# Five gate groups as Strassen-type block products, forgetting softmax divided later, attention's halves added in DRAM: a hybrid decoder block on one core

## The chip, the core and the metric

The kernel runs on one core of a Trainium2 chip. The metric is the time of one execution on the device in microseconds; here it is the median of three runs. The engines work side by side and are named as in the profile: PE (matrix products), PEld (its loads of the stationary operand), DVE and ACT (vector and scalar engines), POOL and SP (which in this kernel mostly issue transfers; POOL also does a few elementwise operations). PSUM holds eight banks of 128 x 512 float32, into which PE writes.

## The reference

One decoder block over 1024 tokens of width 1024. Three attention branches are computed from one normalised input, each is multiplied by a sigmoid gate, and the sum goes through an output projection and a squared-ReLU MLP.

```python
proj = jnp.einsum('bsd,de->bse', h, w_in[l])
sb_q, sb_k, sb_v, fx_q, fx_k, fx_v, f_logit, m_q, gate_logit = split_columns(proj, SPLITS)
o_sb = stick_breaking_attention(...)      # 8 heads of 64
o_fox = forgetting_attention(...)         # 8 heads of 64, causal softmax with a decay
o_mem = memory_attention(mq, mk, ...)     # 4 heads of 128 over 256 memory tokens
gates = jax.nn.sigmoid(gate_logit.reshape(b, s, N_BRANCH, D_MODEL))
merged = gates[:, :, 0] * br_sb + gates[:, :, 1] * br_fox + gates[:, :, 2] * br_mem
x = x + jnp.einsum('bsd,de->bse', merged, w_out[l])
h2 = rmsnorm(x, g_mlp_norm[l])
u = jax.nn.relu(jnp.einsum('bsd,df->bsf', h2, w_ff_up[l]))
x = x + jnp.einsum('bsf,fd->bsd', u * u, w_ff_down[l])
```

`gate_logit` is a product of 1024 tokens x 1024 inputs x 3072 columns. The kernel writes its transpose to DRAM: 24 gates of 128 columns each.

## The kernel before

**Precision.** Every float32 operand is split into a high and a low part (`split`: ACT copies the high part, DVE subtracts), and every product is three matmuls (`passes`, high x high, high x low, low x high).

**Planner.** Up to the last branch, and again in a later part, the program is written as processes (`Op`, `Get`, `Sleep`, events) that a small simulated machine runs while the kernel is built. Each `Op` names an engine and a cost in microseconds; the order in which the machine starts them becomes the order of instructions on that engine. On the chip each engine runs its instructions in that order, each waiting for what it needs. An `Op` marked `side` on PE goes behind all others that are ready: the dense products are filler between attention's. `late` shifts a process's place among those that are ready. `Get` takes a buffer from a list (`Places`) and waits until one is free.

**Stages.** The prologue normalises and transposes the tokens (`hTh`, `hTl`: the transposed input, high and low, as 8 chunks of 128 inputs x 1024 tokens). Then come the values of the forgetting heads, two gates and the memory keys and values. Then six projections (`unit_products`, `PROJ`), each 512 columns, already done in seven block products: the 1024 inputs and 512 columns of the weights and the 1024 inputs and 1024 tokens are cut in halves, sums of the weight blocks (`unit_prep`) and sums of the token blocks (`sums_T`, kept in `T_of` as `P5`, `P6`, `P7`, `P4`) are multiplied in kinds `P1` to `P7`, and the results are added on DVE and ACT. Their weight blocks are loaded on POOL's queue (`unit_loads`, L1322). Then attention: `sb_tile` and `fox_tile` make the weights of one 128-token tile of one head, `unit` turns them on PE, splits them and multiplies them by the values. `load_pairs` loads keys and queries on POOL's queue (L979). Beside attention, on PE, run 22 gates (`dense_gate`, `dense_T`): 2 halves of the tokens x 8 chunks x 3 passes each, their weights loaded (L1037) and split (L1029, L1030) one gate at a time into one of three weight pairs (`WP`); at the opening of pool `A2` one pair is turned into four tiles for attention, and two are left. A gate half is evicted by ACT into an `o` tile (L1530) and stored by SP (L1534). Then the three branches (`dense_branch`, `bring`): memory, stick-breaking, forgetting, each multiplied by its gate, read back from DRAM. Then the output projection and the MLP, which the change does not touch.

**Softmax of the forgetting heads** (`fox_tile`, `fox` in the names): for each chunk of up to 512 keys DVE adds the causal mask to the last 128 columns (L843), takes the maximum (L844) and its negative (L845), and ACT takes the exponential with the sum (L848). With two chunks, small DVE operations (L856 to L867) make a factor for each, and ACT multiplies the whole row by it (L871).

**Attention's output.** The values are a high and a low part beside each other, so the product has 128 rows: 64 of each. ACT copies the low rows (L939), DVE adds the high ones (L940), SP stores the sum (L942).

## Time and profile before

| what | us |
|---|---|
| three runs | 1706.46, 1706.36, 1706.93 |
| the profiled execution | 1706.93 |
| its span, first to last instruction | 1705.1 |
| last store of attention's output, start | 845.4 |
| last store of a gate, start | 851.8 |

The page gives busy time by engine, the span in slices, the chain of work that ended last, and groups of instructions by line, engine and tile, with the mean duration of one and the idle time of the engine in front of them. In a row such as `pp<-hi,whi` the first name is what is written and the others what is read. Matmuls overlap, so the mean duration of one is longer than the distance to the next.

### The profile page before, as it was taken

To read this page: it belongs to the slowest core of one execution; us is meant where nothing else is said; L and a number is where in the kernel's file an instruction comes from. 1 tells how busy PE (TensorE), PEld (TensorE's weight loads), DVE (VectorE), ACT (ScalarE), POOL (GpSimd) and SP (SyncE) were. 2 spreads that over 40 slices of the span, in tenths; PEclk is the share of its full clock that TensorE was granted. 3 is DMA by queue.
4 is the path that set the end of the run, shared out by engine and by line. 5 is a ranking of instruction groups with operands and counts; after the bars stand their busy time and mean duration, and the time that the engine had idled before them with its cause. 6 is when DMAs were issued, how large, how long until landed. Compare 5 with 4: busy or idle time off the path is not lost.

```text
span 1705.1 us, 25350 instructions
## 1 busy us (share of the span) xinstructions
PE 1691.7 (99%) x9186; PEld 1442.8 (85%) x9186; DVE 1346.3 (79%) x2321; ACT 886.8 (52%) x1635; POOL 256.0 (15%) x441
## 2 busy tenths in 40 slices
PE   9999999999999999999999999999999999999998
PEld 9998899998888888888888887878888887888887
DVE  7977678868999888888656898987777776788775
ACT  6445555556676798889733446533233344332331
POOL 0000000043322233241000011021211120000000
PEclk9999999999999999999999999999999999999999
DMA  7545444576544453553375642144444484554532
GB/s 242 162 144 191 135 124 149 157 245 187 160 128 123 113 176 112 183 164 110 100 238 168 217 179 94 56 162 141 156 153 149 142 289 180 195 206 148 198 123 74
DMA packets 131406, 271.72 MB, mean 159 GB/s; under 512 B 15761, under 2 KB 43409, under 8 KB 131281
## 3 DMA queue, kind: packets, MB, share of 16 engines
q1 hardware_dynamic: 99600, 169.94, 29.2%
q0 software_dynamic: 31680, 100.17, 19.5%
q8 instruction: 72, 1.18, 0.3%
q14 instruction: 54, 0.43, 0.1%
HBM read 181.44 MB, written 88.60 MB: 158 GB/s over the span
## 4 chain that ended last, share of the span: by engine, by line
PE 83%; issue 7%; DVE 5%; DMA 2%; POOL 2%; ACT 1%; SPq 0%; POOLq 0%; DVEq 0%; ACTq 0%
PE pp L1119 21%; PE pp L2518 7%; PE pp L1405 7%; PE pp L1848 6%; PE sc L1405 5%; PE tr L904 4%; PE tr L2518 4%; PE sc L2518 4%; PE sc L1119 3%; PE sc L1848 3%; PE pv L2518 2%; PE pv L921 2%; PE pp L921 2%; PE pv L1405 2%; POOL s_scr L1865 2%
## 5 line engine op out<-in xcount | busy, mean ns | idle before, releaser
L1119 PE MATMUL pp<-hi,whi 128*128 128x512 f32 x368 | 147.6, 401 | 0.0
L1119 PE MATMUL pp<-hi,wlo 128*128 128x512 f32 x368 | 145.0, 394 | 0.0
L1119 PE MATMUL pp<-lo,whi 128*128 128x512 f32 x368 | 144.8, 393 | 0.0
L1030 DVE TENSOR_TENSOR wlo<-raw,whi 128x1024 fp32r<-128x1024 f32 (+1 forms) x82 | 100.0, 1221 | 38.9 <-ACT whi L1029 38.6
L2518 PE MATMUL pp<-h,sop 128*128 128x512 f32 x540 | 128.7, 395 | 1.4 <-DVE sop L1784 1.4
L2518 PEld LDWEIGHTS pp<-h,sop 128*128 128x128 f32 x540 | 101.1, 187 | 26.5 <-DVE sop L1784 1.8
L1848 PE MATMUL pp<-h,oh 128*128 128x512 f32 x384 | 120.9, 396 | 0.7 <-ACT cu L1934 0.6
L1029 ACT ACTIVATE whi<-raw 128x1024 fp32r<-128x1024 f32 (+1 forms) x82 | 86.8, 1059 | 52.4 <-PE pp L1405 18.7
L911 DVE TENSOR_TENSOR ptl<-tr,pth 128x512 fp32r<-128x512 f32 (+1 forms) x160 | 98.8, 627 | 11.0 <-ACT pth L909 10.6
L909 ACT ACTIVATE pth<-tr 128x512 fp32r<-128x512 f32 (+1 forms) x160 | 86.7, 558 | 28.5 <-PE tr L904 15.5
L814 DVE TENSOR_TENSOR_SCAN r<-r,sm 128x896 f32<-128x896 f32 (+4 forms) x64 | 85.5, 1345 | 3.5 <-ACT r L799 3.4
L2436 ACT ACTIVATE h<-t 128x2048 fp32r<-128x2048 f32 x16 | 30.7, 1919 | 110.4 <-DVE t L1784 97.9
L1848 PEld LDWEIGHTS pp<-h,oh 128*128 128x128 f32 x384 | 71.7, 187 | 19.2 <-ACT cu L1934 1.5
L1119 PEld LDWEIGHTS pp<-hi,wlo 128*128 128x128 f32 x368 | 69.1, 188 | 16.4
L1119 PEld LDWEIGHTS pp<-lo,whi 128*128 128x128 f32 x368 | 69.5, 189 | 10.3
L1119 PEld LDWEIGHTS pp<-hi,whi 128*128 128x128 f32 x368 | 69.4, 189 | 10.1
L1848 PE MATMUL pp<-h,ol 128*128 128x512 f32 x192 | 75.9, 396 | 0.0
L1841 ACT ACTIVATE oh<-raw 128x512 fp32r<-128x512 f32 x64 | 39.4, 625 | 61.7 <-DVE raw L1784 61.7
L2518 PE MATMUL sc<-h,sop 128*128 128x512 f32 x264 | 63.4, 395 | 0.0
L2518 PE MATMUL tr<-h,sop 128*128 128x512 f32 x264 | 63.4, 395 | 0.0
L1784 DVE TENSOR_TENSOR sop<-ur,sop 128x2048 fp32r<-128x2048 f32 x27 | 61.7, 2286 | 1.7 <-ACT sop L2447 1.7
L844 DVE TENSOR_REDUCE st<-sc 128x1 f32<-128x512 f32 (+2 forms) x96 | 53.3, 555 | 9.3 <-PE sc L838 7.1
(586 smaller groups left out, 5102.9 us busy)
## 6 DMA issues: line engine op xcount, KB each, us to landing
ur<-s_scr SPq DMA_DIRECT2D x26, 1024.0 KB
raw<-w_in POOLq DMA_DIRECT2D x42, 512.0 KB, 5.2
raw<-w_up SPq DMA_DIRECT2D x60, 256.0 KB
s_scr<-s POOLq DMA_DIRECT2D x60, 256.0 KB, 2.5
g<-w_down SPq DMA_DIRECT2D x14, 1024.0 KB
s_scr<-cu POOLq DMA_DIRECT2D x48, 256.0 KB, 2.9
gate_scr<-o SPq DMA_DIRECT2D x44, 256.0 KB
o<-gate_scr SPq DMA_DIRECT2D x32, 256.0 KB
```

The source lines that it names most:

```text
L814: nc.vector.tensor_tensor_scan(out=rev, data0=rev, data1=zero.to_broadcast([P, n]), initial=1.0, op0=ALU.mult, op1=ALU.add)
L904: nc.tensor.transpose(tr[:, jj * 256 + a * P:jj * 256 + (a + 1) * P], es[a][:, j * P:(j + 1) * P], ident)
L909: yield Op("ACT", act_time(512 - lo_c), lambda: nc.scalar.activation(ph[:, lo_c:], tr[:, lo_c:], AF.Copy))
L911: yield Op("DVE", dve_time(512 - lo_c), lambda: nc.vector.tensor_tensor(pl[:, lo_c:], tr[:, lo_c:], f32(ph[:, lo_c:]), ALU.subtract))
L921: nc.tensor.matmul(pv[0][:, c_:256], pair.v[:, j, b, :], p_[:, jj * 256 + c_:(jj + 1) * 256], start=(k == 0 and n_ == 0 and i == 0), stop= ...
L1029: yield Op("ACT", 0.03 + act_time(m), lambda: nc.scalar.activation(hi, raw, AF.Copy))
L1030: yield Op("DVE", dve_time(m), lambda: nc.vector.tensor_tensor(lo, raw, f32(hi), ALU.subtract))
L1119: nc.tensor.matmul(ps, a_, b_, start=(first and i == 0), stop=(last and i == n - 1))
L1405: nc.tensor.matmul(out_, a_, b_, start=(first and n == 0 and j == 0), stop=(last and n == 3 and j == len(todo) - 1), skip_group_check=True)
L1784: nc.vector.tensor_tensor(out_, a_, b_, op)
L1848: nc.tensor.matmul(ps, w[a_][:, k * P:(k + 1) * P], h[b_][k], start=(first and k == 0 and i == 0), stop=(last and k == 3 and i == 2), skip ...
L2518: nc.tensor.matmul(ps, a_[:, c, qs], b_[:, c, :], start=(kind in ("P1", "P2", "P7") and c == 0 and i == 0), stop=(kind in ("P2", "P4", "P3 ...
```

## The change

**Gates.** Of the 24 gates, 20 form five groups of 512 columns (`GATES`); two others (10 and 11) stay as they were, and gates 8 and 9 are done earlier as before. A group is done in seven block products of 2 x 4 x 3 = 24 matmuls (`gate_unit`), in three stages over all five groups: `P2` of all; then `P5` and `P3`; then `P1`, `P6`, `P7` and `P4`. Within a stage the kinds of one group accumulate in the same two banks, and after each kind ACT copies the running sum out (`evicted`), which is stored in the gate array by SP, or added to it by an accumulating transfer on POOL. The quarters of `hTh` and `hTl` that a stage has used up are overwritten with the token sums (`bring_T`), which were kept in DRAM (`keep_T`). The sums of weight blocks are made in DRAM beforehand (`gate_sums`): copies and accumulating transfers on POOL, with a load, a change of sign on ACT and a store where a block is subtracted.

**Gate sigmoids.** The gates of the memory branch were passed through the sigmoid at eviction; now they are stored without it, and it is applied when they are read back.

**Softmax.** Scores of the forgetting heads come negated (the sign moves into the query gain and the decay), so that a minimum gives the bias of the exponential directly; mask and minimum of the last chunk are one DVE instruction. The second chunk waits for the first one's minimum and uses the common one; the first is corrected by one DVE product over 512 columns. The rows are no longer divided by their sums: the reciprocals are stored (`sums_kept`), and `bring` of the forgetting branch loads them spread over 64 rows each and multiplies the attention output by them.

**Halves.** ACT copies all 128 rows of the output; SP stores the two halves to two arrays, and when a pair of heads is over, one accumulating transfer on POOL adds the low array to the other (`pair.added`).

**Buffers.** `bring` takes its raw tile from `RR` in place of `RAW`, and its first two tiles no longer wait for the branch to be chosen.

The core of the diff:

```diff
+    GATES, DIVIDED = (4, 5, 0, 1, 3), ()
...
+    def sums_kept(h0):
+        cols = fn[:, 8 * h0:8 * h0 + 16]
+        yield Op("DVE", SMALL, lambda: nc.vector.reciprocal(cols, cols))
+        yield Op("SP", 0.4, lambda: nc.sync.dma_start(
+            l_scr[h0:h0 + 2, :].rearrange("h (i p) -> p (h i)", p=P), cols, allow_slow_non_contiguous=True), 4.0)
...
             def maxima():
                 if c + u == n:
-                    dg = sc[:, u - P:u]
-                    nc.vector.tensor_tensor(dg, dg, tri, ALU.add)
-                nc.vector.tensor_reduce(mx[:, ci:ci + 1], sc[:, :u], AX.X, ALU.max)
-                nc.vector.tensor_scalar(nx[:, ci:ci + 1], mx[:, ci:ci + 1], -1.0, None, ALU.mult)
+                    nc.vector.tensor_tensor_reduce(sc[:, :u], sc[:, :u], holder["later"][:, 512 - u:512], 1.0, -NEG,
+                                                   ALU.add, ALU.min, nx[:, ci:ci + 1])
+                else:
+                    nc.vector.tensor_reduce(nx[:, ci:ci + 1], sc[:, :u], AX.X, ALU.min)
...
+            if ci == 0:
+                machine.fire(first_max)
+            else:
+                yield first_max
+                bias = m
+                yield Op("DVE", SMALL, lambda: nc.vector.tensor_tensor(m, nx[:, 0:1], nx[:, 1:2], ALU.min))
...
-        yield Op("DVE", SMALL * (4 if two else 1), scale)
-        yield Op("ACT", act_time(*[u for _, _, u in ch]) + 0.0002 * n, scaled)
+            def scaled():
+                nc.vector.tensor_scalar(e[:, :512], e[:, :512], f, None, ALU.mult)
+                nc.vector.scalar_tensor_tensor(total, l[:, 0:1], f, l[:, 1:2], ALU.mult, ALU.add)
+            yield Op("DVE", dve_time(512) + SMALL, scaled)
...
-        yield Op("ACT", act_time(256), lambda: nc.scalar.activation(o, pv[0][HD:P, :256], AF.Copy))
-        yield Op("DVE", dve_time(256), lambda: nc.vector.tensor_tensor(o, o, pv[0][0:HD, :256], ALU.add))
+        yield Op("ACT", act_time(256), lambda: nc.scalar.activation(ob, pv[0][:, :256], AF.Copy))
...
+            rows = slice(pair.p * P, pair.p * P + P)
+            yield Op("POOL", 0.8, lambda: nc.gpsimd.dma_start(
+                scr[rows, :], low_scr[pair.kind != "sb"][rows, :], max_dma_last_dim=2048, accum_op=ALU.add), 4.0)
+            machine.fire(pair.added)
...
+    def gate_sums():
+        yield kv_over
+        def moved(dst, src, **kw):
+            yield Op("POOL", 0.9, lambda: nc.gpsimd.dma_start(dst, src, max_dma_last_dim=2048, **kw), 0.0)
+            yield Sleep(7.5)
+        def turned(u, key, dst):
+            raw = yield Get(RAW)
+            view = raw[:, :1024].rearrange("p (k n) -> p k n", k=4)
+            yield from moved(view, gate_block(u, key).rearrange("(k p) n -> p k n", p=P))
+            yield Op("ACT", act_time(1024), lambda: nc.scalar.activation(raw[:, :1024], raw[:, :1024], AF.Copy, scale=-1.0))
+            yield Op("SP", 0.1, lambda: nc.sync.dma_start(dst.rearrange("(k p) n -> p k n", p=P), view), 6.0)
+            RAW.put(raw)
+        def first(u):
+            yield from moved(ws_scr[u, "P5"], gate_block(u, "21"))
+            yield from moved(ws_scr[u, "P5"], gate_block(u, "22"), accum_op=ALU.add)
+        def rest(u):
+            s3, s2, s4 = (ws_scr[u, k] for k in ("P7", "P6", "P3"))
+            two = [spawn(turned(u, "21", s3)), spawn(turned(u, "22", s2))]
+            yield two[0]
+            yield from moved(s3, gate_block(u, "11"), accum_op=ALU.add)
+            yield two[1]
+            yield from moved(s2, s3, accum_op=ALU.add)
+            yield from moved(s4, s2)
+            yield from moved(s4, gate_block(u, "12"), accum_op=ALU.add)
+        evs = []
+        for u in GATES:
+            evs += [spawn(first(u)), spawn(rest(u))]
+            yield Sleep(25.0)
...
+        def evicted(kind, q, ps, last, snapped):
+            yield last
+            gt = yield Get(OO)
+            yield Op("ACT", act_time(512), lambda: nc.scalar.activation(gt, ps, AF.Copy))
+            machine.fire(snapped)
+            if kind == kinds[-1]:
+                PP.put(ps)
+            (c, t), add = TO[kind]
+            r0 = u * 512 + c * 256 + q * P
+            dst = gate_scr[r0:r0 + P, t * 512:(t + 1) * 512]
+            if add:
+                yield Sleep(1.0)
+                yield Op("POOL", 0.9, lambda: nc.gpsimd.dma_start(dst, gt, accum_op=ALU.add), 4.0)
+            else:
+                yield Op("SP", 0.1, lambda: nc.sync.dma_start(dst, gt), 2.7)
+            OO.put(gt)
...
+                for q in range(2):
+                    if j == 0:
+                        banks_.append((yield Get(PP)))
+                    else:
+                        yield snapped[q]
...
-    gates = [dense_gate(n, may_gate) for n in (*range(16, 24), *range(0, 8), *range(10, 16))]
+    plain = [dense_gate(n, may_gate) for n in (*range(16, 24), *range(0, 8), *range(10, 16)) if n // 4 not in GATES]
+    stage = [[gate_unit(u, kinds, may_gate if i == 0 else (lambda: sums_in.fired)) for u in GATES]
+             for i, kinds in enumerate((("P2",), ("P5", "P3"), ("P1", "P6", "P7", "P4")))]
+    gates = plain + stage[0] + stage[1] + stage[2]
...
+        spawn(gate_sums(), -10.0)
+        spawn(keep_T(), 2.0)
+        spawn(bring_T("P5", plain))
+        spawn(bring_T("P6", stage[0]))
+        spawn(bring_T("P7", stage[1]))
+        spawn(bring_T("P4", stage[1]))
```

215 lines of the change are left out of this document (161 added, 54 removed).

## The prediction

> **What bounds the kernel now.** I read the page first, then the windows of busy time by stage, then the lines and waits of the one stage that the change touches.
>
> ```profile
> span 1705.1 us, 25350 instructions
> PE 1691.7 (99%) x9186; PEld 1442.8 (85%) x9186; DVE 1346.3 (79%) x2321; ACT 886.8 (52%) x1635; POOL 256.0 (15%) x441
> PE 83%; issue 7%; DVE 5%; DMA 2%; POOL 2%; ACT 1%; SPq 0%; POOLq 0%; DVEq 0%; ACTq 0%
> ...
> 115.00:365.00 250.00, 250.00 (x1800) 234.53 (x1799) 194.72 (x354) 129.39 (x205) 22.85 (x34) 1.00 0.49 155
> 365.00:600.00 235.00, 234.03 (x1355) 202.49 (x1354) 211.93 (x340) 164.96 (x357) 79.90 (x140) 1.00 0.54 155
> 600.00:851.00 251.00, 251.00 (x1514) 218.91 (x1513) 205.28 (x642) 212.21 (x546) 70.69 (x126) 1.00 0.46 140
> 851.00:1060.00 209.00, 207.29 (x908) 167.35 (x907) 162.99 (x241) 94.59 (x151) 16.81 (x17) 1.00 0.53 180
> ```
>
> The columns of a window row are its length, then PE, weight loads, DVE, ACT and POOL busy, the granted clock, the DMA share and GB/s. The first row is the projections, the next two are the attention stage (stick-breaking, then forgetting and memory attention), with the gates as filler on PE, and the last is the branches. PE is without a gap in all of them, at the full clock of 1.00. So one matmul less is worth its spacing, as long as nothing else opens a gap. The next engines are close: in the attention stage DVE is busy 417.2 of 486 us (86%, and 90% in its first half), ACT 377.2 us (78%).
>
> ```profile
> L942 SPq DMA_DIRECT2D o_scr<-ob x64: 445/446/559, 390.1 to 845.4; - x64
> ...
> L1534 SPq DMA_DIRECT2D gate_scr<-o x44: 319/326/328, 372.0 to 851.8; - x44
> ```
>
> These are the transfers that store the attention's outputs and the gates, with the start of the first and of the last. Attention ends at 845.4, the gates at 851.8: they end together. Attention's matmuls go first by the planner, so its pace is that of DVE and ACT, and the gates take what is left of PE. To end earlier, both must shrink.
>
> **The gates' products.** The gates' matmuls in this stage, and the spacing of twelve of them in the chain of waits:
>
> ```profile
> L1119 PE MATMUL pp<-hi,whi 128*128 128x512 f32 x352 | 141.3, 401 | 0.0
> L1119 PE MATMUL pp<-hi,wlo 128*128 128x512 f32 x352 | 138.7, 394 | 0.0
> L1119 PE MATMUL pp<-lo,whi 128*128 128x512 f32 x352 | 138.5, 393 | 0.0
> ...
> 366.20 2.78 PE pp L1119 x12
> ```
>
> 1056 matmuls are 22 gates of 48, at 2.78 / 12 = 0.232 us each (the mean of 0.39 to 0.40 us is a duration that overlaps its neighbours). A group of 512 columns costs 4 x 48 = 192 of them; by block products it costs 7 kinds x 2 halves x 12 = 168. Five groups save 5 x 24 = 120 matmuls, 120 x 0.232 = **27.8 us** of PE. No other stage loses or gains a matmul.
>
> **What the vector engines gain and lose in this stage.** The rows that go, and the two that price what comes:
>
> ```profile
> L844 DVE TENSOR_REDUCE st<-sc 128x1 f32<-128x512 f32 (+2 forms) x96 | 53.3, 555 | 9.3 <-PE sc L838 7.1
> L1030 DVE TENSOR_TENSOR wlo<-raw,whi 128x1024 fp32r<-128x1024 f32 x22 | 26.7, 1216 | 1.3 <-ACT whi L1029 1.2
> L843 DVE TENSOR_TENSOR sc<-sc,above 128x128 f32<-128x128 f32 x64 | 18.7, 292 | 6.8 <-PE sc L838 5.7 <-ACT pth L909 0.8
> ...
> L845 DVE TENSOR_SCALAR st<-st 128x1 f32<-128x1 f32 x96 | 14.7, 154 | 3.3
> L940 DVE TENSOR_TENSOR ob<-ob,pv 64x256 f32<-64x256 f32 x33 | 13.4, 405 | 7.6 <-ACT ob L939 7.5
> L940 DVE TENSOR_TENSOR ob<-ob,pp 64x256 f32<-64x256 f32 x31 | 12.4, 402 | 3.1 <-ACT ob L939 3.1
> ...
> L636 DVE TENSOR_SCALAR r<-r,st 128x256 f32<-128x256 f32 x32 | 9.5, 359 | 0.3
> L865 DVE TENSOR_SCALAR st<-st 128x2 f32<-128x2 f32 x32 | 7.3, 229 | 1.1
> L864 DVE RECIPROCAL st<-st 128x1 f32<-128x1 f32 x32 | 5.3, 164 | 1.1
> L863 DVE TENSOR_TENSOR st<-st 128x1 f32<-128x1 f32 x32 | 5.1, 160 | 1.1
> L867 DVE RECIPROCAL st<-st 128x1 f32<-128x1 f32 x32 | 4.9, 154 | 1.4 <-ACT es L848 1.4
> L862 DVE TENSOR_TENSOR st<-st 128x2 f32<-128x2 f32 x32 | 4.8, 151 | 2.5 <-ACT st L858 2.5
> ...
> L616 DVE TENSOR_SCALAR st<-st 128x2 f32<-128x2 f32 x16 | 2.8, 176 | 0.5
> ```
>
> DVE loses L843, L845, L940, L862 to L867 and L616: 18.7 + 14.7 + 25.8 + 27.4 + 2.8 = 89.4 us. It gains 15 more weight splits (35 blocks and 2 plain gates for 22 gates), 15 x 1.216 = 18.2; 32 products of 128x512 by a column, at 0.49 us by the slope between L865 (2 elements, 229 ns) and L636 (256, 359), or 0.68 if they run like a two-operand instruction of that size: 15.7 to 21.8; 32 small ones like L865, 7.3. The reduction that now adds the mask is not in the trace: between nothing (one instruction like L844) and 0.2 us (a separate read of the result, which ACT's row below has) on 64 tiles, 0 to 13; I take 6. Sum 41 to 60, so DVE goes down by 29 to 48 us, to 369 to 388. Over a stage of 486 - 28 = 458 us that is 81 to 85%: no worse than now.
>
> ```profile
> L871 ACT ACTIVATE e<-e,st 128x512 f32<-128x512 f32 x64 | 37.6, 639 | 2.7 <-DVE st L865 1.8 <-DVE st L856 0.6
> ...
> L1530 ACT ACTIVATE o<-pp 128x512 f32<-128x512 f32 x43 | 25.8, 601 | 13.3 <-PE pp L1119 13.2
> L1029 ACT ACTIVATE whi<-raw 128x1024 fp32r<-128x1024 f32 x22 | 23.4, 1063 | 3.8 <-DMA raw<-w_in 3.8
> L871 ACT ACTIVATE es<-es,st 128x128 f32<-128x128 f32 (+3 forms) x32 | 17.7, 561 | 0.6 <-DVE st L867 0.5
> ...
> L848 ACT ACTIVATION_READ_ACCUMULATOR e<-sc,st 128x1 f32 x64 | 12.8, 201 | 0.0
> ```
>
> ACT loses L871, 55.3 us, and gains 30 evictions (74 for 44), 18.0, and 15 splits, 15.9: 355.8 us, 78% of 458, as now. The relief lies in the forgetting half (DVE there loses some 76 us and gains 35); in the stick-breaking half L940's 12.9 us pays just for some ten more splits, so that half keeps its pace and the gates move 385 of their 936 matmuls into the second, which has 251 - 555 x 0.232 + 48 x 0.232 (memory attention's own 48 matmuls, by the code, are also on L1119) = 133 us of attention on PE and 89 us of gates, 222 for 251. Should attention lag behind the gates all the same, branch 0 (192 matmuls, 44.5 us, with operands from memory attention alone) fills PE. I cost the relief itself at nothing beyond the 27.8: PE sets the end. Without that relief DVE would be at 417 + 18 = 435 of 458 us, 95%, and attention would last as now.
>
> **The weights' cadence.** Three weight pairs exist, and one of them is given to attention's tiles, so two serve the gates. A pair in use for 48 matmuls now serves 24.
>
> ```profile
> 463.28 0.60 ACT L1530 ACTIVATE o<-pp 128x512 f32<-128x512 f32 x1 [0.32 <-PE pp L1119]
> ...
> 470.26 1.22 DVE L1030 TENSOR_TENSOR wlo<-raw,whi 128x1024 fp32r<-128x1024 f32 x1
> ...
> 365.00:600.00 235.00, 144.33 (x551) 1.00 0.54 155
> 600.00:851.00 251.00, 148.27 (x555) 1.00 0.46 140
> ```
>
> A gate's last matmul releases its pair at 463.3, and the pair is split again at 471.5: 8.2 us. L1119 takes 551 x 0.232 = 128 of 235 us in the first half, so a block of 24 (5.57 us alone) lasts 10.3 us there, and 13.9 in the second half (89 of 222). The refill fits with 2 us to spare. Bounds: nothing, and 1.2 us for each of 23 blocks (a refill of 11.5 us behind 30 more evictions), 28 us. I take **3 us**, near the measured refill.
>
> **The transfers in the projections.** The weight sums run on POOL from about 115 us on, the partial sums of the tokens on SP. Per group: 2 loads, 2 stores, 2 copies and 4 adding transfers of 512 KB; 26.2 MB for five groups, and 8.4 MB of token sums. ACT's ten sign changes (10 x 1.063) are hidden in its 121 us of idle time there.
>
> ```profile
> L1322 POOL DMA_DIRECT2D raw<-w_in x20 | 15.2, 760 | 282.5 <-DVE wlo L1030 282.5
> ...
> DMA to landing us min/median/max: 4.1/4.9/6.2
> ...
> 307.12 0.75 POOL L1322 DMA_DIRECT2D raw<-w_in  x1 [6.27 <-DVE wlo L1030]
> ...
> 319.09 1.21 DVE L1335 TENSOR_TENSOR s<-raw,raw 128x1024 f32<-128x1024 f32 x1
> ```
>
> What is queued behind them on POOL are the blocks of the projections' weights (L1322, the first two rows); the last two rows are the last block's issue and its first use, 12 us apart, so a landing of 4.9 us has 7 us to spare. The engines carry 155 GB/s at a share of 0.49, so 316 when full; 34.6 MB in 250 us are 138 GB/s, which makes a share of 0.93. No adding transfer is in the trace. Its cost is bounded by a plain one (4.9 us) from below, and from above by twice the bytes, a share of 1.06, with which the sums simply end later: their first use, after 2 plain gates and the five P2 blocks, is at about 365 + 41 + 51 = 457. The sums have time; what can be late are the blocks, by nothing or by 7 us a unit in 5 units (the slow rival). I take **3 us**.
>
> The Trainium skill, "Collectives: The Full Stack", section "The bandwidth ceiling: the fold count and why AG ≠ RS ≠ AR", says that an add in the transfer path needs two source reads and runs at half the rate of a copy. By it 4.9 us become an estimated 9.8; no run here shows it yet, and it is the side on which the slow rival lies.
>
> In the attention stage POOL gets 15 loads, 30 adding stores and 8 pair adds, 53 x 0.76 = 40 us on 151 busy, in 458: hidden in its waits. The last pair's add delays only branch 2's operand, with branches 0 and 1 in front of it. The 16 sigmoids of branch 0's gates (16 x 0.6) and its broadcast sums lie in the branch window, where ACT has 114 us idle.
>
> **Sum.** The profiled execution took 1706.93 us (span 1705.1, 1.8 around it; the median of the runs is 0.5 lower): 1706.9 - 27.8 + 3 + 3 = **1685 us**.
>
> **The rivals.** *Nothing lost*: 1679 us, the bare 27.8. For it: PE has no gap now. Against: twice the weight blocks and 53 more transfers in POOL's order.
>
> *The cadence decides*: each kind waits for its weights. If half of the 28 us bound comes true, 1706.9 - 27.8 + 14 + 3 = 1696; up to 1704 with more of it. For it: 2 us of room, DVE at 90% in the first half. Against: POOL issues loads well ahead, and the order of ACT and DVE is planned around them.
>
> *The blocks of the projections are late*, the case on the other side: adding transfers, each waiting on POOL for the landing of the one it depends on, hold back L1322, and a full set of DMA engines stretches its landing. It decides from a landing past 12 us; at 19 us each of the 5 later units waits 7, 35 us in all: 1706.9 - 27.8 + 35 = 1714. For it: the share of 0.93 to 1.06 if all runs in that stage. Against: POOL waits 282 us on this stage for releases, room for 40 issues, and the sums may run on until 457.
>
> *No effect*: the 27.8 come back as gaps at the end because attention paces the stage. Branch 0 as filler speaks against it; it would be 1706.
>
> **How the numbers follow.** Forecast, 1680 to 1692: 0.55. Nothing lost, below 1680: 0.08. Cadence, 1692 to 1705: 0.15. No effect: 0.02. Late blocks, above 1710: 0.20. A measurement of this kernel tells about 0.2% (3.4 us) from no change: faster 0.76 (all of the first three but 0.02), same 0.04, slower 0.20. The range 1677 to 1708 leaves out the slow rival.
>
> **What would show it.** Right: 936 matmuls in the gates' groups, PE without gaps until about 823 and the branches as before; DVE below 390 us in the attention stage; L1322 landing below 12 us. Wrong: PE idle in front of weight blocks with DVE's split as releaser (cadence); PE idle between 115 and 365 with L1335 behind a block's landing (late blocks); PE idle after the last gate while attention still stores (attention paces).

## The result, and the profile after

The changed kernel takes **1760.9 us** (median of four executions; 1752.5 to 1769.3), beside 1706.7 for the kernel before: 1.0314 times as long, with a 95% interval of 1.0294 to 1.0335. The forecast was 1685. The execution profiled here took 1764.6 us. From its page:

```profile
span 1762.9 us, 25226 instructions
...
PE 1686.6 (96%) x9066; PEld 1435.7 (81%) x9066; DVE 1311.5 (74%) x2072; ACT 877.8 (50%) x1610; POOL 336.7 (19%) x534
...
DMA packets 176894, 340.97 MB, mean 193 GB/s; under 512 B 27072, under 2 KB 71616, under 8 KB 175744
...
PE 72%; DMA 13%; DVE 6%; issue 4%; ACT 3%; POOL 2%; SPq 0%; ACTq 0%; POOLq 0%; DVEq 0%
```

The 120 matmuls are gone (9186 to 9066), but PE's busy time fell by 5.1 us and not by 27.8, and PE is idle 1762.9 - 1686.6 = 76.3 us where it was idle 13.4. In the chain of waits DMA has 13%, where it had 2%. So the span grew by 62.9 us of idle PE and fell by 5.1. The windows by stage, with the columns of the prediction's first fence, say where PE was idle and where its clock was lower:

```profile
115.00:365.00 250.00, 231.16 (x1594) 213.94 (x1593) 183.53 (x327) 130.21 (x198) 52.09 (x64) 0.97 0.89 250
365.00:600.00 235.00, 231.40 (x1427) 203.90 (x1427) 205.56 (x302) 165.09 (x360) 87.11 (x152) 1.00 0.77 233
600.00:851.00 251.00, 223.21 (x1320) 193.83 (x1320) 162.03 (x402) 167.62 (x447) 104.72 (x167) 0.94 0.82 190
851.00:920.00 69.00, 57.48 (x286) 46.83 (x285) 32.88 (x69) 36.29 (x79) 10.94 (x13) 0.93 0.85 164
```

PE lost 18.8 us in the projections and 39.3 us between 600 and 920 (27.8 and 11.5). No other engine is near its limit there: DVE is busy 65% between 600 and 851, ACT 67%. The granted clock is below 1.00 in the same stages: 1686.6 - (1691.7 - 27.8) = 22.7 us is what the same matmuls took more. The DMA share is 0.77 to 0.89, and between 600 and 920 at *fewer* GB/s than between 365 and 600. That is the first thing to look at.

**Four stores that fill the DMA engines.** The store of the reciprocals of the row sums, and the same execution in windows of 5 us around the first two of the four:

```profile
L603 SPq DMA_DIRECT2D l_scr<-fn x4: 376/378/387, 691.2 to 888.5; - x4
```

```profile
685.00:690.00 5.00, 5.00 (x32) 4.43 (x32) 4.96 (x13) 4.14 (x11) 5.00 (x11) 1.00 0.75 227
690.00:695.00 5.00, 5.00 (x30) 4.33 (x29) 3.36 (x12) 3.67 (x12) 3.11 (x5) 1.00 1.29 112
695.00:700.00 5.00, 5.00 (x33) 4.33 (x32) 3.67 (x9) 3.54 (x11) 3.59 (x6) 1.00 0.73 21
700.00:705.00 5.00, 3.47 (x23) 2.73 (x21) 0.75 (x2) 0.38 (x2) 0.52 (x1) 1.00 0.95 181
705.00:710.00 5.00, 0.99 (x5) 0.99 (x6) 1.49 (x2) 2.86 (x8) 1.57 (x3) 0.69 1.05 233
710.00:715.00 5.00, 5.00 (x18) 4.24 (x18) 4.02 (x12) 2.22 (x6) 2.30 (x5) 0.63 0.96 313
...
765.00:770.00 5.00, 2.88 (x17) 2.12 (x15) 1.31 (x5) 0.00 (x0) 0.94 (x2) 1.00 0.82 139
770.00:775.00 5.00, 0.00 (x0) 0.00 (x0) 0.00 (x0) 0.08 (x1) 2.44 (x4) 0.67 1.08 315
775.00:780.00 5.00, 2.43 (x6) 1.85 (x7) 2.89 (x5) 3.85 (x9) 0.00 (x0) 0.50 1.08 310
```

The store is issued at 691.2. For the next ten microseconds the DMA share (last column but one) stays at 1.29 and 0.73 while the engines move 112 and then 21 GB/s. Then the engines stop: from 700 on DVE and ACT do next to nothing, and soon PE too, idle for 1.5 and 4.0 us of two windows. It comes back at a clock of 0.63, so 18 matmuls fill a window that held 30 and more before. The second gap, at 770, is 9.7 us of three windows, with a clock of 0.50 in the last. Each gap is paid twice, as idle time and then as slow matmuls. The Trainium skill, "TensorE: Matmul & The Clock Gate", Part 1, says that an idle window of about 3.4 us takes the clock to half. These rows agree: the clock reads 0.50 behind the gap of 9.7 us.

How a late store stops engines that have nothing to do with it is in the chain of waits of that stretch (start, length, what):

```profile
693.31 13.75 DMA o_scr<-o
...
707.14 0.21 ACT o L685
...
707.64 0.60 ACT pth L918
...
708.26 0.70 DVE ptl L920
...
709.01 0.90 PE tr L913 x3
```

A store of 256 KB of the memory branch, next on SP's queue, lands after 13.75 us. ACT waits for its tile (L685) to copy the next bank; behind it in ACT's fixed order is attention's copy (L918), behind that DVE's split (L920), behind that PE's turn (L913), for which PE waits 5.5 us. The next matmuls of the gates stand behind that turn in PE's order, which is written down too. The second gap has the same form with another transfer: ACT waits 10.3 us to split a gate's weight block that has not landed, and PE waits 9.7 us for attention's exponential behind it.

**The projections.** The issue line of the weight blocks of the projections with their time to landing, the chain of waits in this stage, two instructions of ACT with the idle time in front of them (in brackets, with what ended it), the waits of PE between 115 and 365 (us in all, how often, the longest), and three windows of 10 us:

```profile
L1356 POOL DMA_DIRECT2D raw<-w_in x20: 748/780/1589, 131.2 to 336.1; - x20
...
DMA to landing us min/median/max: 4.5/8.1/13.9
```

```profile
176.09 0.75 POOL raw L1580
176.84 15.85 DMA raw<-w_in
...
192.71 0.03 ACT raw L1587
...
212.29 12.10 DMA raw<-w_in
...
243.53 11.09 DMA raw<-w_in
```

```profile
191.34 1.06 ACT L1587 ACTIVATE raw<-raw 128x1024 f32<-128x1024 f32 x1 [8.89 <-DMA raw<-w_in]
...
253.26 1.06 ACT L1587 ACTIVATE raw<-raw 128x1024 f32<-128x1024 f32 x1 [5.97 <-DMA raw<-w_in]
```

```profile
PE sc L1439 <- ACT sn L1478: 9.5, 1, 9.5
PE tr L716 <- DVE sn L708: 7.0, 3, 4.0
PE pp L1439 <- DVE wlo L1057: 0.9, 1, 0.9
PE pp L1153 <- DVE wlo L1057: 0.9, 1, 0.9
PE pp L1153 <- ACT whi L1056: 0.6, 1, 0.6
```

```profile
190.00:200.00 10.00, 0.78 (x2) 0.69 (x3) 2.51 (x4) 7.45 (x8) 3.22 (x4) 0.74 1.12 283
250.00:260.00 10.00, 5.98 (x38) 5.78 (x37) 4.55 (x14) 6.58 (x12) 3.13 (x4) 0.83 1.08 256
300.00:310.00 10.00, 10.00 (x88) 10.00 (x87) 9.73 (x23) 4.59 (x9) 0.00 (x0) 1.00 0.12 40
```

The blocks of the projections, which landed in 4.9 us, land in 8.1 (13.9 at most). But they are not what stops PE. The three transfers that hold the chain for 11 to 16 us are loads of the weight sums themselves (issued on L1580; the tile is named `raw` there too), and what waits for them is ACT's change of sign (L1587). In ACT's fixed order the projections' own work stands behind it. At 191 ACT has waited 8.9 us, then comes to the copy of a finished product out of PSUM (L1478), and PE, which needs that bank, has waited 9.5 us. At 253 ACT has waited 6.0 us, DVE's L708 needs a root that ACT takes behind it, and PE has waited 4.0. These two are 13.5 of the 18.8 us that PE lost in this stage; for split weight blocks it waited 2.4 us in all (the last three rows of its waits). The DMA share is 0.84 to 1.14 while the sums run and 0.12 at 300, when they are done: the stage's mean of 0.89 hides a full stretch with a much emptier one behind it.

### The profile page after: what moved, and what is told of

The parts are those of the page before. It is cut to its first block, busy times and chain, and to the rows that moved or that the text cites. A ratio compares the mean times of both kernels' runs of the same rounds, so it can differ in the third digit from the quotient of the medians.

```text
span 1762.9 us, 25226 instructions
## 1 busy us (share of the span) xinstructions
PE 1686.6 (96%) x9066; PEld 1435.7 (81%) x9066; DVE 1311.5 (74%) x2072; ACT 877.8 (50%) x1610; POOL 336.7 (19%) x534
## 2 busy tenths in 40 slices
DMA packets 176894, 340.97 MB, mean 193 GB/s; under 512 B 27072, under 2 KB 71616, under 8 KB 175744
## 4 chain that ended last, share of the span: by engine, by line
PE 72%; DMA 13%; DVE 6%; issue 4%; ACT 3%; POOL 2%; SPq 0%; ACTq 0%; POOLq 0%; DVEq 0%
PE pp L2056 9%; PE pp L1705 8%; PE pp L2726 7%; PE pp L1153 5%; PE sc L2056 4%; DMA raw<-w_in 4%; PE pp L1439 4%; PE tr L2726 3%; PE sc L2726 3%; PE sc L1153 3%; PE sc L1439 3%; DMA gate_scr<-o 3%; PE tr L913 3%; PE pv L2726 2%; PE tr L2056 2%
## 5 line engine op out<-in xcount | busy, mean ns | idle before, releaser
L1057 DVE TENSOR_TENSOR wlo<-raw,whi 128x1024 fp32r<-128x1024 f32 (+1 forms) x92 | 112.3, 1221 | 74.9 <-ACT whi L1056 74.8
L920 DVE TENSOR_TENSOR ptl<-tr,pth 128x512 fp32r<-128x512 f32 (+1 forms) x160 | 99.3, 630 | 37.2 <-ACT pth L918 35.2
L1056 ACT ACTIVATE whi<-raw 128x1024 fp32r<-128x1024 f32 (+1 forms) x92 | 97.4, 1060 | 57.3 <-DMA raw<-w_in 19.5
L1705 PE MATMUL pp<-hi,whi 128*128 128x512 f32 x280 | 114.6, 409 | 0.0
L1705 PE MATMUL pp<-hi,wlo 128*128 128x512 f32 x280 | 112.4, 401 | 0.7 <-DVE wlo L1057 0.7
L1705 PE MATMUL pp<-lo,whi 128*128 128x512 f32 x280 | 111.9, 400 | 0.0
L918 ACT ACTIVATE pth<-tr 128x512 fp32r<-128x512 f32 (+1 forms) x160 | 87.5, 566 | 31.5 <-PE tr L913 13.3
L825 DVE TENSOR_TENSOR_SCAN r<-r,sm 128x896 f32<-128x896 f32 (+5 forms) x64 | 85.5, 1348 | 3.2 <-ACT r L809 2.9
L913 PE MATMUL tr<-ident,e 128*128 128x128 f32 x416 | 62.6, 279 | 3.6 <-DVE ptl L920 3.0
L1673 ACT ACTIVATE o<-pp 128x512 f32<-128x512 f32 x70 | 42.2, 604 | 45.6 <-PE pp L1705 25.7
L1705 PEld LDWEIGHTS pp<-hi,wlo 128*128 128x128 f32 x280 | 53.6, 191 | 13.9 <-DVE wlo L1057 1.1
L2073 POOL DMA_DIRECT2D s_scr<-cu x48 | 26.0, 542 | 193.8 <-DVE cu L2063 190.0
## 6 DMA issues: line engine op xcount, KB each, us to landing
ws_P<-w_in POOLq DMA_DIRECT2D x20, 512.0 KB, 10.3
```

The source lines that it names most:

```text
L825: nc.vector.tensor_tensor_scan(out=rev, data0=rev, data1=zero.to_broadcast([P, n]), initial=1.0, op0=ALU.mult, op1=ALU.add)
L913: nc.tensor.transpose(tr[:, jj * 256 + a * P:jj * 256 + (a + 1) * P], es[a][:, j * P:(j + 1) * P], ident)
L918: yield Op("ACT", act_time(512 - lo_c), lambda: nc.scalar.activation(ph[:, lo_c:], tr[:, lo_c:], AF.Copy))
L920: yield Op("DVE", dve_time(512 - lo_c), lambda: nc.vector.tensor_tensor(pl[:, lo_c:], tr[:, lo_c:], f32(ph[:, lo_c:]), ALU.subtract))
L1056: yield Op("ACT", 0.03 + act_time(m), lambda: nc.scalar.activation(hi, raw, AF.Copy))
L1057: yield Op("DVE", dve_time(m), lambda: nc.vector.tensor_tensor(lo, raw, f32(hi), ALU.subtract))
```

## The experiments

Every ratio is to the kernel before, run beside it on the same chip. Steps between two runs are differences of ratios times 1706.7 us.

| run | median us | ratio, 95% interval |
|---|---|---|
| the changed kernel | 1760.9 | 1.0314 [1.0294, 1.0335] |
| e1 row sums turned on PE | 1723.5 | 1.0107 [1.0092, 1.0122] |
| e16 row sums in rows of 32 bytes | 1724.7 | 1.0101 [1.0084, 1.0118] |
| e2 no weight sums | 1739.4 | 1.0194 [1.0167, 1.0222] |
| e5 ordinary gate stores | 1746.3 | 1.0235 [1.0216, 1.0254] |
| e6 = e1 and no weight sums | 1708.2 | 1.0006 [0.9996, 1.0016] |
| e9 = e6 and ordinary gate stores | 1700.3 | 0.9963 [0.9949, 0.9977] |
| e13 = e6, token sums planned, not sent | 1698.1 | 0.9952 [0.9937, 0.9967] |
| e10 = e6 and no token sums | 1685.0 | 0.9869 [0.9849, 0.9889] |
| e11 = e10 and ordinary gate stores | 1683.1 | 0.9866 [0.9838, 0.9895] |
| e3 no block products | 1704.9 | 0.9992 [0.9982, 1.0001] |
| e7 = e3, row sums turned | 1705.7 | 0.9999 [0.9989, 1.0009] |
| e17 = e3, rows of 32 bytes | 1702.4 | 0.9982 [0.9973, 0.9992] |
| e4 = e1, weight sums at half pace | 1712.4 | 1.0036 [1.0019, 1.0053] |
| e8 = e4, token transfers spread | 1713.4 | 1.0038 [1.0023, 1.0053] |
| e14 = e4, token loads on ACT's queue | 1722.5 | 1.0095 [1.0080, 1.0110] |
| e15 = e4, planned for earlier landings | 1742.5 | 1.0218 [1.0200, 1.0235] |
| e12 = e4, planned for later landings | 1770.3 | 1.0365 [1.0338, 1.0392] |

### The row sums: e1 and e16

e1 turns the sixteen columns first, so that rows of 512 bytes are stored:

```diff
-            l_scr[h0:h0 + 2, :].rearrange("h (i p) -> p (h i)", p=P), cols, allow_slow_non_contiguous=True), 4.0)
...
+        yield Op("PE", 0.12, lambda: nc.tensor.transpose(tr[:16, :P], cols, ident))
...
+        yield Op("ACT", act_time(P), lambda: nc.scalar.activation(ob[:16, :P], tr[:16, :P], AF.Copy))
...
+            l_scr[h0:h0 + 2, :].rearrange("h (i p) -> (h i) p", p=P), ob[:16, :P]), 2.5)
```

> The changed kernel with one edit: the 16 columns of row sums are turned on PE, copied by ACT and stored as rows of 512 bytes, in place of the four stores of 4-byte elements. Theory A (each of the four stores holds the DMA engines for about 15 us, attention's own store behind it lands after 13.75 us, PE stands some 10 us and then runs at a granted clock of 0.5 to 0.7): the four gaps at 691, 755, 822 and 889 us go, about 12 us each with the clock, 48 in all: 1761 - 48 = 1713 us, clock back to 0.99 or more in the attention stage. Theory B (the weight sums fill the DMA engines in the projections, 16 us of PE idle there and as much again by the clock): this run changes nothing before 600 us, and the 16 us of idle between 140 and 300 stay. Rival (the gaps after 690 come from the gates' accumulating stores and the pair adds): they stay, 1755 to 1761 us.

e1 gained 2.07%, 35 us, where theory A had 48; the rival is out. Theory B held in so far as PE still loses 17 us in the projections. But the new steps made the planner write another order on every engine, so e16 was added later, with one line other and the order of all engines as it was:

```diff
-            l_scr[h0:h0 + 2, :].rearrange("h (i p) -> p (h i)", p=P), cols, allow_slow_non_contiguous=True), 4.0)
+            l_scr[h0:h0 + 2, :].rearrange("h (p i) -> p h i", p=P), cols.rearrange("p (h i) -> p h i", h=2)), 4.0)
```

> The changed kernel with one line other: the four row-sum stores write the same 8 KB each in rows of 8 elements (32 bytes), so 256 pieces for 2048, and the row sums lie in another order. Order and waits of all engines are those of the changed kernel. Theory A (the 2048 small pieces of each store): 1761 - 37 = 1724 us, DMA share behind the stores below 1.1, no gap at 705, 770, 825 and 905. Rival (the other order that the planner wrote for the turned row sums): 1752 us or more.

e16 gained 2.13%, **36 us**, from the same bytes in the same place. Its page, and the windows behind its first store (issued at 694.2):

```profile
DMA packets 169726, 340.97 MB, mean 198 GB/s; under 512 B 19904, under 2 KB 64448, under 8 KB 168576
```

```profile
695.00:700.00 5.00, 5.00 (x31) 4.33 (x30) 3.61 (x12) 4.41 (x14) 3.11 (x6) 1.00 0.93 189
700.00:705.00 5.00, 5.00 (x37) 4.52 (x35) 3.53 (x7) 3.80 (x10) 2.62 (x5) 1.00 1.02 240
705.00:710.00 5.00, 5.00 (x28) 4.26 (x27) 4.71 (x12) 3.44 (x10) 1.66 (x4) 1.00 1.05 299
```

There are 176894 - 169726 = 7168 packets less, which is 4 x (2048 - 256): each store was cut into one packet for each 4-byte element. With 256 pieces the engines carry 189 to 299 GB/s behind it and PE has no gap. The Trainium skill, "DMA: Bandwidth & Descriptors", "Rules for kernel authors", says that a last dimension that is not contiguous lowers to one descriptor per element; this run agrees and gives the price in this kernel.

### Without block products: e3, e7, e17

```diff
-    GATES, DIVIDED = (4, 5, 0, 1, 3), ()
+    GATES, DIVIDED = (), ()
...
-        spawn(gate_sums(), -10.0)
-        spawn(keep_T(), 2.0)
...
```

> The changed kernel with all gates computed plainly, so without block products, weight sums and token sums; the softmax relief, the pair adds in DRAM and the four row-sum stores stay. 120 matmuls of 0.232 us come back. Theory A: the projections are as in the kernel before and the four gaps are there: 1707 + 40 to 48 = 1747 to 1755 us. Rival (the gaps come from the gates' accumulating stores, which this run has not): no gaps, 1700 to 1708 us.

> The softmax relief and the pair adds alone, with turned row sums, all gates computed plainly. Theory (the four stores of 4-byte elements cost 3 us where the attention stage has room): 1704.9 - 3 = 1702 us, PE without the two gaps near 717 and 777. Rival (the relief is worth much and the stores hide it, as theory A had it): 1670 to 1680 us. Rival (PE sets the end, the stores cost nothing): 1705 us.

> The run with all gates computed plainly (1704.9 us, four stores of 4-byte elements in it), with the same one line other: rows of 32 bytes, the row sums in another order, all engines' orders as in that run. Theory (the same four stores cost next to nothing where PE has gates of 48 matmuls for each weight pair and little other traffic: two gaps of 1.5 us): 1702 to 1705 us. Rival (they cost here too, hidden by the relief): 1690 us or less.

e3 refuted theory A as it stood: with the same four stores the time is that of the kernel before. Rows of 32 bytes at an unchanged order on every engine gain 0.10%, under 2 us, where they gain 36 in the changed kernel. So the stores are not dear by themselves; they are dear in the kernel with the block products. Which part of those makes them so is not shown: the traffic, a weight pair that serves 24 matmuls in place of 48, or the order. (The adding stores are at most a small part of it: they cost 13 us beside the row-sum stores and 7 without those and the weight sums, as the next runs show.) In the windows of e3, behind its second store (issued at 700.6), the stall is there, and PE loses 1.5 us at a clock that stays at 1.00:

```profile
710.00:715.00 5.00, 5.00 (x33) 4.34 (x32) 3.46 (x10) 3.02 (x9) 1.99 (x3) 1.00 1.00 159
715.00:720.00 5.00, 3.53 (x23) 2.92 (x22) 2.07 (x4) 2.83 (x7) 1.07 (x2) 1.00 1.08 310
```

And the relief of DVE and ACT, with the pair adds in DRAM beside it, is worth nothing that can be told from no change (e7: 0.9999, as its last rival had it).

### The adding stores: e5 and e9

```diff
-                yield Op("POOL", 0.9, lambda: nc.gpsimd.dma_start(dst, gt, accum_op=ALU.add), 4.0)
+                yield Op("POOL", 0.9, lambda: nc.gpsimd.dma_start(dst, gt), 4.0)
```

> The changed kernel in which the gates' 30 adding stores are ordinary stores on the same queue, so the partial results of the gates are not added; the weight sums and the four row-sum stores of 4-byte elements stay. Without block products the same four stores cost 3 us of PE, with them 37. Theory D (the row-sum stores meet the adding stores, and it is the pair that fills the DMA engines: share 1.3 to 1.7 behind them): without adds the four gaps shrink to about 3 us and the time falls by some 30, to 1728 to 1735 us. Rival E (it is the rest: more traffic, and a weight pair that now serves 24 matmuls and not 48, so that the same stall of the DMA engines uncovers PE): the gaps stay, 1752 to 1761 us.

> Turned row sums, no weight sums, and the gates' 30 adding stores as ordinary stores, so the gates' partial results are not added. The run before it without the last edit took 1708 us, of which 16.7 us are PE idle more than in the kernel before and about 9 us matmuls at a lower clock. Theory F (an adding transfer loads the DMA engines more than a plain one of the same bytes, and that is what makes the other transfers late): 6 to 10 us less, 1698 to 1702 us, DMA share between 600 and 851 below 0.70. Rival G (it is POOL's order: the store waits there for its eviction, 92.7 us in all, and the weight blocks and attention's loads queue behind it, added or not): 1706 to 1709 us.

The order of all engines is unchanged in both. Beside the 4-byte stores the adds cost 0.79%, 13 us, less than the 30 expected of theory D, and not the nothing of rival E. Without those stores and the weight sums they cost 0.43%, 7 us, as theory F had it. The spans of e6 and e9, and the time that the packets of POOL's queue took:

```profile
span 1702.9 us, 25163 instructions
...
q0 software_dynamic: 40336, 120.09, 24.6%
```

```profile
span 1693.5 us, 25163 instructions
...
q0 software_dynamic: 38416, 120.09, 23.0%
```

The same 120.09 MB took 0.246 x 1702.9 - 0.230 x 1693.5 = 29.4 us of all 16 engines less: 0.98 us for each of 30 stores. By the prediction's 316 GB/s an ordinary store of 256 KB takes an estimated 0.83 us, so the add about doubles it. The rule that the prediction cited from the Trainium skill, "Collectives: The Full Stack", "The bandwidth ceiling: the fold count and why AG ≠ RS ≠ AR" (an add needs two source reads, which halves its rate beside a copy; stated there for the reducing step of a collective), agrees with it.

### The weight sums: e2, e6, e4

```diff
-                          [(0, gate_block(u, BLOCK[kind]) if kind in BLOCK else ws_scr[u, kind])], 4, 256))
+                          [(0, gate_block(u, BLOCK.get(kind, "21")))], 4, 256))
...
-    stage = [[gate_unit(u, kinds, may_gate if i == 0 else (lambda: sums_in.fired)) for u in GATES]
+    stage = [[gate_unit(u, kinds, may_gate) for u in GATES]
...
-        spawn(gate_sums(), -10.0)
```

With the sums go ACT's ten changes of sign, their loads and stores, and the gates' wait for the sums at build time, so the order on every engine is another one.

> The changed kernel without the weight sums' transfers: the kinds P3, P5, P6 and P7 load a plain block of the weights instead of a sum, so this part of the result is another; the number of loads and of matmuls stays. Theory B: the projections end as before the change (PE without a gap between 115 and 365, DMA share about 0.55), some 25 to 30 us less: 1761 - 27 = 1734 us; the gaps after the row-sum stores stay. Rival (the projections lose nothing that is not made good later, since the sums need not end before 457): 1755 to 1761 us.

> The changed kernel with turned row sums and without the weight sums' transfers (plain blocks of the weights are loaded in place of the sums). Theory B (the two losses lie in different stages and add): 1761 - 37 - 22 = 1702 us, and PE without a gap between 115 and 365. Rival (the traffic of the sums was also what slowed the attention stage): 1690 us or less. Rival (the order of the loads, not their bytes): no gain over 1712.

The gain was 1.20% (20 us) with the row sums as they were and 1.01% (17 us) with them turned, a few us short of theory B in both. In e2 PE is as busy in the projections as in the kernel before:

```profile
115.00:365.00 250.00, 249.60 (x1799) 234.54 (x1799) 196.42 (x355) 129.68 (x204) 23.69 (x36) 1.00 0.51 166
```

e4 keeps the sums, with turned row sums, and issues them at half the pace:

```diff
-            yield Sleep(7.5)
+            yield Sleep(14.0)
...
-            yield Sleep(25.0)
+            yield Sleep(50.0)
```

> The run with turned row sums, and the weight sums issued at half the pace (14 us in place of 7.5 within a group, 50 in place of 25 between groups). Theory A and B together (both stalls gone, the gates' 27.8 us kept, a few us left at the token sums): 1685 to 1695 us, DMA share below 1.0 from 140 to 300. Rival (the sums at this pace come too late for their first use at about 457 and the gates wait): PE idle in the attention stage behind weight blocks, 1715 us or more. If pacing does nothing, as with turned row sums alone: 1713 us.

It gained 0.71%, 12 us, over e1, some two thirds of what leaving the sums out gains, and missed the 1685 to 1695 us of the theory. (It came out near the 1713 us of "pacing does nothing" only because e1 had been forecast there and took 1723.5.) At half the pace the change of sign is planned 14 us behind the issue of its load in place of 7.5; in the trace of e4 ACT waits for none of the ten, and PE loses 4.8 us between 115 and 365. Whether the thinner traffic or the later place in ACT's order did it is not separated. With e8 it is the fastest version with all of the change in it, and still 0.36% slower than before. Where it loses time next is the end of the gates' second stage: the chain of waits, and two windows.

```profile
584.50 17.01 DMA gate_scr<-o
```

```profile
600.00:610.00 10.00, 6.10 (x21) 4.79 (x21) 3.48 (x8) 7.38 (x15) 2.07 (x3) 0.83 0.47 108
610.00:620.00 10.00, 8.02 (x44) 6.68 (x45) 8.88 (x21) 7.32 (x18) 5.49 (x11) 0.83 0.44 106
```

A gate's store is on SP's queue behind four loads of 1 MB of token sums, issued within 3 us, and lands after 17 us; in these two windows PE loses 5.9 us, at a clock of 0.83.

### The token sums: e8, e14, e10, e13, e11

e8 sets these transfers apart from each other, e14 issues the loads from ACT:

```diff
+                yield Sleep(9.0)
...
+        if kind == "P4":
+            yield Sleep(16.0)
...
+            yield from transfer(issue, P * 8192, 0.4)
+            yield Sleep(3.0)
```

```diff
-                nc.sync.dma_start(f32(dst), src)
+                nc.scalar.dma_start(f32(dst), src)
-        yield from transfer(issue, P * 16384, 0.8)
+        yield from transfer(issue, P * 16384, 1.2, queue_="ACT")
```

> Turned row sums and weight sums at half the pace, and in addition the token sums' transfers apart from each other: 9 us between the eight stores of 1 MB, and the last four loads (4 MB that were issued within 3 us at 581) in two pairs, 16 us and more apart. Theory C (the gate's store behind these 4 MB landed after 17.0 us, ACT waited for its tile, PE lost 6 us at 600 to 620 and then ran at a clock of 0.83): 8 us less than 1712, 1700 to 1705 us. Rival (the gap moves to the next burst): 1710 to 1714 us.

> The run with turned row sums and slow weight sums (1712 us), with the eight loads of the token sums issued by ACT on a queue of its own, so that no store of attention or of a gate is behind them. Theory (the place on SP's queue: the gate's store behind 4 MB landed after 17 us): the gap at 600 to 620 goes, and two smaller ones, 1698 to 1704 us. Rival (the bytes themselves slow whatever runs beside them, on any queue): 1708 to 1716 us.

Both theories missed; e8 came out as its rival had it, e14 slower than both. In e8 the gap at 600 went and others came at 640, 680, 700 and 730; the time is e4's. e14 is 10 us slower than e4, and its gap at 600 to 620 is still there (2.0 and 2.8 us of PE). Both edits rewrote the order of the engines, so neither tells what the bytes cost. e10 leaves the sixteen transfers out and e13 keeps their place in the plan without sending them, on top of e6:

```diff
-                yield Op("SP", 0.4, lambda dst=dst, t=t: nc.sync.dma_start(dst, f32(t)), 6.0)
...
-        yield from transfer(issue, P * 16384, 0.8)
-        yield Sleep(2.0)
```

```diff
-                yield Op("SP", 0.4, lambda dst=dst, t=t: nc.sync.dma_start(dst, f32(t)), 6.0)
+                yield Op("SP", 0.4, lambda dst=dst, t=t: None, 6.0)
...
-            for dst, src in zip(quarter(*PLACE[kind]), t_scr[kind]):
-                nc.sync.dma_start(f32(dst), src)
+            pass
```

> Turned row sums, no weight sums, and no transfers of the token sums either (neither the eight stores of 1 MB nor the eight loads; the block products then run on other tokens, same count of matmuls). Theory C: the gaps at 100 to 120 (2.2 us), 410 to 420 (2.3) and 590 to 610 (4.3, with a clock of 0.66 to 0.83 behind it) go: 1708 - 10 = 1698 us. Rival G (POOL's order sets the loss): 1705 to 1709 us.

> Turned row sums, no weight sums; the token sums' sixteen transfers keep their places and times in the order written at build time, but none is sent, so the block products run on other tokens. PE, DVE, ACT and POOL have the very order of the run that took 1708 us. Theory C (the transfers themselves: 2 to 4 MB at once, and the stores behind them on SP's queue): 1683 to 1690 us, as without them. Rival I (the order that is written around their waits): 1704 to 1709 us.

e10 gained 1.37%, 23 us. e13 runs the order of e6 on PE, DVE, ACT and POOL, and gained 0.54%, **9 us**: that is the price of the transfers in that order. The other 0.83%, **14 us**, is the order that the planner writes around them: neither e13 nor e10 sends them. Theory and rival were each right in part. Between 600 and 851, e13 and then e10:

```profile
600.00:851.00 251.00, 244.05 (x1455) 211.07 (x1454) 170.09 (x417) 180.49 (x477) 105.51 (x165) 0.99 0.77 203
```

```profile
600.00:851.00 251.00, 246.73 (x1497) 214.88 (x1496) 178.97 (x438) 184.76 (x490) 109.07 (x172) 1.00 0.80 212
```

e10 carries *more* GB/s at a higher share and loses less PE. So a higher share does not by itself cost PE more.

e11 is e10 with ordinary gate stores:

> Turned row sums, no weight sums, no token sums, ordinary stores in place of adding ones: of the gates' change only the 120 matmuls less, the 24 instead of 48 matmuls for each weight pair, the 30 more evictions and their stores on POOL stay. If transfers' bytes and adds are all that eats the gain: 1706 - 27.8 + 3 to 6 = 1681 to 1685 us, clock 1.00. Rival G (the order on POOL and the twice as frequent weight blocks eat part by themselves): 1690 to 1700 us. If nothing of the 27.8 us comes out here: 1704 or more.

```profile
span 1677.7 us, 25145 instructions
...
PE 1664.2 (99%) x9070; PEld 1420.9 (85%) x9070; DVE 1311.1 (78%) x2072; ACT 869.4 (52%) x1604; POOL 292.6 (17%) x494
...
600.00:851.00 251.00, 251.00 (x1512) 218.93 (x1511) 181.48 (x438) 188.11 (x495) 96.60 (x167) 1.00 0.71 216
```

Here the gain is whole in the profiled execution: PE is busy 1664.2 us, the forecast's 1691.7 - 27.8 = 1663.9, and idle 13.5 us as before the change. That execution took 1679.5 us; the median of four is 1683.1, inside the first of the ranges expected, and 1.34% or 23 us below the kernel before. The step from e10 to e11 (0.03%) is too small to be told.

### The order written at build time: e12 and e15

```diff
-        yield Sleep(machine.pipe + 2.0 - machine.now)
+        yield Sleep(machine.pipe + (4.0 if kv_over.fired else 2.0) - machine.now)
```

with a lower rate and longer landings of the stores beside it in e12; e15 turns all of them the other way (1.0 and a higher rate).

> The run with turned row sums and slow weight sums (1712 us), with the same work and one more edit: the order written at build time now counts landings as they were measured (a block of 512 KB 7 us in place of 4, an adding store 9 in place of 4, a gate's store 6 in place of 2.7, the halves 6 in place of 3). Theory H (the order on each engine is fixed for landings of 4 us, and each one that lands at 7 to 17 us stops an engine): gaps of PE shrink by half, 1698 to 1704 us. Rival (the engines are simply full at a share of 0.75 to 0.90): 1709 to 1714 us.

> The run with turned row sums and slow weight sums (1712 us), with the order written for earlier landings (a block of 512 KB 2.3 us in place of 4, adding stores 2 in place of 4). Later landings in the plan cost 58 us. Theory H' (a plan that waits less leaves fewer holes in PE's order): 1700 to 1708 us. Rival (the plan with the right size of landing is best, each way off costs): 1716 us or more.

Both theories missed, and in one direction: 3.3% (56 us) and 1.8% (31 us) longer than e4, with the same work. For e15 that is the side of its rival, each way off costs; but e12, which planned nearer the measured landings, did worst. It counted 7 us for a block and 9 for an adding store; in e4's trace, between 365 and 920, the medians from issue to landing are 7.4 and 4.8. Why the plan with 4 and 4 does best is open.

## Why the prediction was wrong, by its steps

From the changed kernel to e11 the single steps are 35 (row sums), 17 (weight sums), 9 and 14 (token sums, transfers and order) and 1 us (adds, once the rest is gone). Together they are 76 us: but for rounding, the 54 lost and the 23 gained. The prices hold for this order of steps; the adds alone cost 13, 7 or 1 us, by what else was left out.

- **The list of what the change adds** failed first. The store of the reciprocals was in the diff, with its flag for a slow layout, and in no term of the sum 1706.9 - 27.8 + 3 + 3. Four transfers of 8 KB cost 36 us at an unchanged order (e16). Nothing in the trace of before had such a store, so it should have had a bound from both sides, like the reduction with the mask.
- **"Hidden in its 121 us of idle time"**, said of ACT's ten sign changes, failed in the projections, and with it "I take 3 us", which was mis-sized: leaving the weight sums out gains 17 to 20 us, though at another order. The step counted the 1.06 us that each change of sign is busy, and not that ACT, at its place in the order, waits for the load: 15.3 us in all, and PE 13.5 us behind two of these waits. The slow rival had the stage and the direction right and the mechanism wrong. Its sign, L1335 behind a block's landing, is not in the trace (the line is L1369 there, and waits for no load), and split weight blocks held PE for 2.4 us only. That its 1714 lies near e1's 1723 is luck. The mean misled as well: 34.6 MB over 250 us gave a share of 0.93 and the stage shows 0.89, but the sums ran at 0.84 to 1.14 and were over by 300. (Six of the eight token stores were issued before 115, and belong to an earlier stretch.)
- **"Hidden in its waits"** for 53 transfers of the attention stage counted POOL's time to issue them, and not what they do to the DMA engines. There the adds cost 7 to 13 us (e9, e5). The eight loads of the token sums were counted in no stage; stores, loads and the order around them cost 23 (e10).
- **The clock** was taken as staying at 1.00. Of the loss, 22.7 us are matmuls that took longer at a lower one.
- **The order** was not a term at all, and differences of 14 to 56 us came from it, at the same work (e13 and e10; e15 and e12).
- **Right**: the matmuls' 27.8 us (e11); the relief at nothing beyond (e7); DVE's sum, 29 to 48 us forecast for the attention stage and 1346.3 - 1311.5 = 34.8 seen over the whole run; the adding transfer near twice a plain one; and the cadence of two weight pairs as small: e11 keeps the 30 evictions and twice the weight blocks, PE waits 1.1 us for a split in its attention stage, and it stands 4.9 us (about 5 either way) above the full gain by the median, where 3 were taken.
- **Small readings** that are off and change nothing: PE had gaps of 1.0 and 1.7 us in the second and fourth window of the first fence, and a block of 24 lasts 10.2 us in the first half, not 10.3.

That late transfers and not a full engine stop PE is shown by e16, e5, e9 and e13, at unchanged orders. For the weight sums it rests on the waits in the trace and on e2, e6 and e4, which all change the order. How the rest of e4's loss divides between transfers and order is not shown.

## What to carry to other kernels

Count a change's transfers by their pieces as well as their bytes, and price every store whose last dimension is not contiguous, however small. Price a transfer by what queues behind it, and at the pace at which it is issued, not by a stage's mean. On engines that run a fixed order, one late landing can stop them all, and on PE the gap is paid again in clock. So an operation put on an engine with idle time is free only if its operand is there when its turn comes: count its wait and not just its busy time. And before an edit's difference is read as its price, look whether the order stayed the same.

## What the runs showed of the hardware that was not expected

- 8 KB in 2048 packets kept the DMA engines at shares of 1.29 and 0.73 for ten microseconds at 112 and 21 GB/s, and a store of 256 KB behind them took 13.75 us; in 256 packets it did not show.
- The same four stores cost 36 us in the kernel with the gates' block products and under 2 us in the one without them (e16, e17).
- A gap of 9.7 us on PE brought the granted clock to 0.50, one of 5.5 us to 0.63, each as the mean of a window of 5 us; one of 1.5 us left it at 1.00 (e3). Lower clocks made the changed kernel's matmuls 22.7 us longer.
- A DMA share of 0.80 at 212 GB/s between 600 and 851 cost PE 4 us (e10), and 0.82 at 190 GB/s cost 28 (the changed kernel): the share alone does not tell a harmless load from a harmful one.
